# Forget gates of a two-layer attention trunk: which operand stands still, and which PSUM pool takes the result

## The chip, the core and the metric

One core of a Trainium2 chip runs the whole kernel. The metric is the device time of one execution in microseconds (us), of which the median of three runs is given. Engine names are those of the profile: PE is TensorE's matmul, PEld its weight load, DVE is VectorE, ACT ScalarE, POOL GpSimd, SP SyncE, which issues the DMAs.

## What is computed

A trunk of two layers over 2048 tokens with 1024 features. Layer 0 normalises each token, projects it, and runs two groups of attention heads on the result: A (differential attention, four heads) and B (forgetting attention, eight heads). Layer 1 does the same with two other kinds of heads. This case is about the forget gates of B: eight numbers for each token, the last eight columns of layer 0's input projection.

```python
def forgetting_attention(q, k, v, log_f):
    cum = jnp.transpose(jnp.cumsum(log_f, axis=1), (0, 2, 1))
    ...
        s = jnp.einsum("bqhd,bkhd->bhqk", qb, k).astype(jnp.float32) * scale
        s = s + cq[..., :, None] - cum[:, :, None, :]
...
def even_layer(x, ln_g, w_in, w_out, ...):
    z = rms_norm(x, ln_g) @ w_in
    aq, ak, av, ag, bq, bk, bv, bg, bf = split_cols(z, EVEN_SPLITS)   # bf: 8 columns
    ...
    log_f = jax.nn.log_sigmoid(bf.astype(f32) + b_f_bias.astype(f32))
```

## The kernel before, in words

The tokens are cut into 16 blocks of 128 (NT). A block's normalised features are split into a high and a low fp16 half and transposed by DMA, so that `st["x"]` is a tile of 128 features x 16 slices x 128 tokens: slices 0 to 7 (KB is 8) are the high halves, 8 to 15 the low ones. Eight blocks (0, 1, 2, 4, 6, 8, 10, 12; the set RES) stay in SBUF under the name `xr`; the others go to DRAM as `xs` and are loaded back as `x` into two buffers, on SP's queue.

The program is a list of steps, one for each unit (a group of heads) and block. A step has pieces: `p` projects a block (`proj`, L235: 24 matmuls of 512 columns, lines 242 to 244, into the pool `pz`) and ends with `post` (evacuation, norm of q and k, split), `q` multiplies queries and keys (`qk_row`, L322; L339) and `v` multiplies weights and values. `drive` (L842) emits the pieces of neighbouring steps interleaved: `merge` (L47) sorts them by a time that it works out from the cost that each piece carries as a number. From what is emitted, the tile framework's scheduler then makes the order of each engine.

Unit A of head 0 runs first, over the stretch up to about 250 us, while the blocks are still being normalised (`norm_x`, L207), and it alone carries the gates. After the 24 matmuls of a block's projection, `forget` (L736) multiplies the gate weights `wf` (128 features x 8 slices x 16 columns: the high and the low half of eight heads) with the block: for each of the eight slices `wf` is loaded as the 16 stationary columns, and both halves of the block, 256 columns, move. The result, 16 x 256, stands in a tile `psf` of the PSUM pool `pT`. In `post`, `forget_gate` (L745) adds the two halves on DVE (L748, into `fg`, 16 x 128), PE transposes `fg` back into the same PSUM tile (L749), DVE adds the two halves of the weights (L751, into `ff`, 128 x 8), and L752 applies scale and bias. The sixteen results feed `log_gates` (L754) and `cumulate` (L764) some steps later.

Two PSUM pools matter. `pT` has one buffer. It also holds `ptq`, the transposes of q and k that follow in `post` (L277 and L281) and that ACT copies out as `kT` and `qT` (L283 and L286); a tile of this pool can be written only when the one before it has been read. `pS` has two buffers of 1024 columns for the scores `pss` (L339), which DVE adds a bias to and reduces to a minimum (L351, result `mx`). The queue of x is shared with the loads `wrn` of raw weights (L953), whose single buffer ACT must have squared (L176) before the next load starts.

Of the kernel before, what the change touches and what calls it, by code (L numbers as in the profile page):

```python
# [9 lines left out]
F32 = mybir.dt.float32  # L10
# [5 lines left out]
ALU = mybir.AluOpType  # L16
AX = mybir.AxisListType

P = 128
# [3 lines left out]
KB = DM // P  # L23
# [36 lines left out]
class Trunk:  # L60
# [365 lines left out]
    def unit_A(self, h, W, wsc, X):  # L426
        nc, ap = self.nc, self.ap
        ks, vs = [], []

        def mk(tb):  # L430
            st = {}
            m = tb + 1

            def p():
                def z():
                    if "z" not in st:
                        st["z"] = self.pz.tile([P, 512], F32, tag="z", name="z")
                    return st["z"][:]
                pieces = self.proj(st, z, W, 512)
                if h == 0:  # L440
                    pieces.append((KB * 0.107, lambda: self.forget(st)))

                def post():
                    z = self.evac(st["z"], 512, wsc())
                    kd = self.ktile(ks, tb)
                    g = self.qk_prep(st, z, 2, 2, self.gA[h], kd)
                    if h == 0:
                        self.forget_gate(st, tb)
                    next(g)
                    vs.append(self.v_split(z[:, 256:384], wsc(), 1))  # L450
                    st["gate"] = self.silu2(z[:, 384:512], self.subg[:])
                    next(g)
                    st["fin"] = g
                return pieces + [(0.34, post)]
# [35 lines left out]
            def v():  # L490
# [20 lines left out]
                pieces.append((0.0, end))  # L511
                return pieces
            return Step(st, lambda: X(st, tb), p, q, v)
        return [mk(tb) for tb in range(NT)]

# [220 lines left out]
    def forget(self, st):  # L736

        nc = self.nc
        ps = st["f"] = self.pT.tile([P, 512], F32, tag="t", name="psf")
        for kb in range(KB):  # L740
            x = st["x"][:, kb::KB]
            nc.tensor.matmul(ps[0:16, 0:256].rearrange("p (a t) -> p a t", a=2), self.wf[:, kb].rearrange("p a h -> p (a h)"), x,
                             start=(kb == 0), stop=(kb == KB - 1))

    def forget_gate(self, st, tb):  # L745
        nc, ps = self.nc, st["f"]
        g = self.sm.tile([16, P], F32, tag="fg", name="fg", bufs=1)
        nc.vector.tensor_reduce(out=g[:], in_=ps[0:16, 0:256].rearrange("p (a t) -> p t a", a=2), axis=AX.X, op=ALU.add)  # L748
        nc.tensor.transpose(ps[:, 256:272], g[:], self.idf[0:16, 0:16])  # L749
        f = self.sm.tile([P, 8], F32, tag="ff", name="ff", bufs=2)  # L750
        nc.vector.tensor_reduce(out=f[:], in_=ps[:, 256:272].rearrange("p (a h) -> p h a", a=2), axis=AX.X, op=ALU.add)  # L751
        nc.vector.scalar_tensor_tensor(out=self.fy[:, tb], in0=f[:], scalar=self.wfsc[:, 0:1], in1=self.bf[:], op0=ALU.mult, op1=ALU.add)  # L752

    def log_gates(self):  # L754
# [391 lines left out]
```

## Time and profile before

| | us |
|---|---|
| median of 3 runs | 2675.35 (2674.71 to 2675.85) |
| profiled execution | 2674.25 |
| its span in the trace | 2672.5 |
| PE busy | 2357.1 (88%) |
| ACT busy | 1861.9 (70%) |
| DVE busy | 1854.3 (69%) |

The busy shares are averages over the whole program. A view by stretches shows where an engine is full and where it stands idle, and the waits of one stretch say for what. The profiled execution took 1.1 us less than the median; 1.75 us of it lie outside its span.

### The profile page before, as it was taken

How to read it: one execution, taken by the hardware profiler on the slowest of the kernel's cores; microseconds unless marked ns; L12 is line 12 of the kernel's file. 1: busy time of each engine (PE TensorE's matmuls, PEld its weight loads, DVE VectorE, ACT ScalarE, POOL GpSimd, SP SyncE). 2: the span in 40 equal slices, each digit the busy share in tenths (PEclk: the TensorE clock that was granted, in tenths of full speed). 3: DMA queues.
4: the chain of work that ended last, by engine and by line, in shares of the span. 5: the costliest groups of instructions: out<-in, count | busy, mean ns of one | idle time of the engine just before them, and what ended most of it. 6: DMA issues, size and time to landing. Idle time of an engine off the chain costs nothing. (4 is left out here: it accounts for less than half of the span.)

```text
span 2672.5 us, 53354 instructions
## 1 busy us (share of the span) xinstructions
PE 2357.1 (88%) x18448; PEld 1300.2 (49%) x18448; DVE 1854.3 (69%) x5228; ACT 1861.9 (70%) x4289; POOL 1463.9 (55%) x2311
## 2 busy tenths in 40 slices
PE   6778888988889989888995898899999999999799
PEld 2344544545455555445553433565555554555344
DVE  6677888888897867857767544566877676767431
ACT  6676777777777877868777444777987777777420
POOL 4555867777786555645554100656575767576300
PEclk9798999999999999999997999999999999999899
DMA  7756555445356997978879999444666776666983
GB/s 213 185 152 137 123 129 132 96 103 125 93 127 133 186 198 147 210 152 165 169 152 193 268 273 245 144 95 118 146 171 138 174 143 163 142 128 141 247 226 103
DMA packets 888208, 426.67 MB, mean 160 GB/s; under 512 B 785377, under 2 KB 816097, under 8 KB 887937
## 3 DMA queue, kind: packets, MB, share of 16 engines
q1 hardware_dynamic: 887936, 423.27, 69.2%
q8 instruction: 144, 2.36, 0.4%
q14 instruction: 128, 1.04, 0.1%
HBM read 187.68 MB, written 42.01 MB: 86 GB/s over the span
## 5 line engine op out<-in xcount | busy, mean ns | idle before, releaser
L374 ACT ACTIVATE row<-row,mx 128x1024 f32<-128x1024 f32 (+7 forms) x512 | 438.2, 857 | 113.2 <-DVE mx L351 111.1
L339 PE MATMUL pss<-kT,qT 128*128 128x512 f16 (+3 forms) x1728 | 398.1, 347 | 56.3 <-DVE mx L351 49.7
L303 DVE SCALAR_TENSOR_TENSOR ph<-row,ph 128x1024 f16<-128x1024 f32 (+6 forms) x320 | 285.6, 902 | 109.3 <-ACT ph L302 107.3
L242 PE MATMUL z<-w,xr 128*128 128x512 f16 x896 | 346.2, 388 | 16.2 <-DMA xr<-xhl 9.0
L242 PE MATMUL z<-w,x 128*128 128x512 f16 x896 | 342.9, 383 | 11.6 <-DMA x<-xs 10.5
L243 PE MATMUL z<-w,xr 128*128 128x512 f16 x896 | 347.2, 388 | 3.4 <-POOL w L113 1.9
L244 PE MATMUL z<-w,xr 128*128 128x512 f16 x896 | 346.4, 387 | 0.0
L243 PE MATMUL z<-w,x 128*128 128x512 f16 x896 | 342.4, 382 | 0.0
L244 PE MATMUL z<-w,x 128*128 128x512 f16 x896 | 342.2, 382 | 0.0
L121 POOL TENSOR_TENSOR y<-v,mhalf 128x4 f32<-128x4 f32 (+2 forms) x329 | 308.4, 938 | 9.1
L407 PE MATMUL OT<-V,pT 128*128 128x64 f16 x5688 | 237.0, 196 | 79.5 <-DMA pT<-ph 77.4
L407 PEld LDWEIGHTS <-pT 128*128 128x128 f16 x5688 | 215.7, 100 | 147.5 <-DMA pT<-ph 96.9
L302 ACT ACTIVATE ph<-row 128x1024 f16<-128x1024 f32 (+6 forms) x320 | 234.4, 744 | 64.0 <-DMA pT<-ph 59.0
L339 PEld LDWEIGHTS <-qT 128*128 128x128 f16 x1728 | 153.1, 101 | 185.9 <-issue 75.7
L273 POOL TENSOR_TENSOR hl<-zs,hl 128x256 f16<-128x256 f32 (+1 forms) x240 | 177.6, 740 | 101.1 <-ACT hl L272 99.2
L123 DVE TENSOR_TENSOR q<-y 128x4 f32<-128x4 f32 (+2 forms) x329 | 90.6, 276 | 204.3 <-POOL y L121 202.4
L272 ACT ACTIVATE hl<-zs 128x512 f16<-128x512 f32 (+1 forms) x240 | 145.8, 608 | 58.9 <-POOL zs L269 52.9
L250 ACT ACTIVATE zs<-z,sc 128x512 f32<-128x512 f32 (+1 forms) x240 | 158.2, 661 | 25.3 <-PE z L244 25.0
L242 PE MATMUL zo<-w,xm 128*128 128x512 f16 x352 | 137.9, 392 | 31.7 <-DVE res L727 14.0
L176 ACT ACTIVATE wrn<-wrn,lng 128x512 f32<-128x512 f32 (+1 forms) x112 | 78.6, 702 | 108.4 <-DMA wrn<-in_wd_dram 43.3
L497 PE MATMUL OA<-V,pT 128*128 128x128 f16 x1632 | 117.4, 230 | 40.6 <-DMA pT<-ph 34.7
L113 POOL TENSOR_TENSOR w<-wraw,w 128x512 f16<-128x512 f32 x118 | 145.6, 1237 | 11.3 <-ACT w L109 10.6
(225 smaller groups left out, 5562.7 us busy)
## 6 DMA issues: line engine op xcount, KB each, us to landing
x<-xs SPq DMA_DIRECT2D x112, 512.0 KB, 3.8
wraw<-in_w_dram SPq DMA_DIRECT2D x64, 256.0 KB, 3.0
wrn<-in_w_dram SPq DMA_DIRECT2D x56, 256.0 KB, 2.9
x<-in_x_dram SPq DMA_DIRECT2D x16, 512.0 KB, 5.1
xs<-xt SPq DMA_DIRECT2D x16, 512.0 KB, 3.3
mixa<-out SPq DMA_DIRECT2D x128, 64.0 KB, 2.1
biasB<-cumd SPq DMA_DIRECT2D x32, 256.0 KB, 5.1
wrn<-in_wo_dram SPq DMA_DIRECT2D x32, 256.0 KB, 3.3
```

The lines of the kernel that those rows point to most:

```text
L121: nc.gpsimd.tensor_tensor(out=y[:], in0=v[:], in1=self.mhalf[:, :n], op=ALU.pow)
L242: nc.tensor.matmul(ps(), xh, wh, start=(kb == 0), stop=False)
L243: nc.tensor.matmul(ps(), xh, wl, start=False, stop=False)
L244: nc.tensor.matmul(ps(), xl, wh, start=False, stop=(kb == KB - 1))
L250: self.nc.scalar.activation(zs[:, :n], z[:, :n], AF.Copy, scale=sc[:, 0:1])
L272: nc.scalar.activation(hl[:, :, 0::2], zn[:, :, None, :].broadcast_to([P, n, 2, 64]), AF.Copy)
L273: nc.gpsimd.tensor_tensor(out=hl[:, :, 1], in0=zn, in1=hl[:, :, 0], op=ALU.subtract)
L302: nc.scalar.activation(hl[:, :n], w, AF.Copy, scale=scale)
L303: nc.vector.scalar_tensor_tensor(out=hl[:, n:2 * n], in0=w, scalar=scale, in1=hl[:, :n], op0=ALU.mult, op1=ALU.subtract)
L339: nc.tensor.matmul(ps, q()[:, j, :], k[:, slot, (b % 4) * P:(b % 4 + n) * P], start=(j == 0), stop=(j == 1 and not (end and diag)), skip_g ...
L374: nc.scalar.activation(row[:, :hm * P], row[:, :hm * P], AF.Exp, scale=-1.0, bias=nmax, accum_out=s[:, i:i + 1])
L407: nc.tensor.matmul(O[:, head], w()[:, a], V()[:, b], start=first and a + b == 0, stop=last and a == 1, skip_group_check=True)
```

## The change

Stationary and moving operand change places. For each of the 16 slices of a block, the slice itself is loaded as 128 stationary columns (tokens), and the 16 columns of the gate weights move. The result comes out with tokens as rows, 128 x 16, with the sum over both halves of the block made in PSUM. So the first sum on DVE (L748) and the transpose on PE (L749) are gone. The tile `psf` comes from the score pool `pS` in place of `pT`, and the cost with which `merge` places the piece falls from 8 x 0.107 to 8 x 0.056.

```diff
-                    pieces.append((KB * 0.107, lambda: self.forget(st)))
+                    pieces.append((KB * 0.056, lambda: self.forget(st)))
...
     def forget(self, st):
         nc = self.nc
-        ps = st["f"] = self.pT.tile([P, 512], F32, tag="t", name="psf")
-        for kb in range(KB):
-            x = st["x"][:, kb::KB]
-            nc.tensor.matmul(ps[0:16, 0:256].rearrange("p (a t) -> p a t", a=2), self.wf[:, kb].rearrange("p a h -> p (a h)"), x,
-                             start=(kb == 0), stop=(kb == KB - 1))
+        ps = st["f"] = self.pS.tile([P, 16], F32, tag="s", name="psf")
+        for k in range(2 * KB):
+            nc.tensor.matmul(ps[:], st["x"][:, k], self.wf[:, k % KB].rearrange("p a h -> p (a h)"), start=(k == 0), stop=(k == 2 * KB - 1))

     def forget_gate(self, st, tb):
         nc, ps = self.nc, st["f"]
-        g = self.sm.tile([16, P], F32, tag="fg", name="fg", bufs=1)
-        nc.vector.tensor_reduce(out=g[:], in_=ps[0:16, 0:256].rearrange("p (a t) -> p t a", a=2), axis=AX.X, op=ALU.add)
-        nc.tensor.transpose(ps[:, 256:272], g[:], self.idf[0:16, 0:16])
         f = self.sm.tile([P, 8], F32, tag="ff", name="ff", bufs=2)
-        nc.vector.tensor_reduce(out=f[:], in_=ps[:, 256:272].rearrange("p (a h) -> p h a", a=2), axis=AX.X, op=ALU.add)
+        nc.vector.tensor_reduce(out=f[:], in_=ps[:].rearrange("p (a h) -> p h a", a=2), axis=AX.X, op=ALU.add)
         nc.vector.scalar_tensor_tensor(out=self.fy[:, tb], in0=f[:], scalar=self.wfsc[:, 0:1], in1=self.bf[:], op0=ALU.mult, op1=ALU.add)
```

The scheduler makes another order from this, on all engines, over the whole of layer 0; the order of layer 1 stays as it was but for some rows. Lines after the edit stand five lower in the changed file (L742 became L741, L751 became L746, L953 L948, L980 L975).

First place, PE, around the scores of block 2 in unit A (`pss`, 128 x 384, lines 339). Before; what is left out are further matmuls of the same kind:

```order
L742 LDWEIGHTS wf [waits PE_49]
L742 MATMUL psf<-x,wf 16x256 [waits Activation_49]
...
L339 LDWEIGHTS qT
L339 MATMUL pss<-kT,qT 128x384
...
L749 MATMUL psf<-idf,fg 128x16 [waits DVE_49]
L277 LDWEIGHTS hl [waits Pool_49]
L277 MATMUL ptq<-idh,hl 128x128 [waits DVE_49]
```

PE waited at the gate product for ACT (the copy `qT`, which frees `pT`), then ran the scores, then waited for DVE twice, once before each kind of transpose.

The same place in the changed program:

```order
L339 LDWEIGHTS qT [waits Activation_49]
L339 MATMUL pss<-kT,qT 128x384 [waits DVE_49]
...
L277 LDWEIGHTS hl [waits Pool_49]
L277 MATMUL ptq<-idh,hl 128x128 [waits PE_49]
...
L339 MATMUL pss<-kT,qT 128x384 [waits DVE_49]
...
L741 LDWEIGHTS xr
L741 MATMUL psf<-wf,xr 128x16 [waits DVE_49]
...
L497 LDWEIGHTS pT [waits DMAHW3_49]
```

The wait for ACT now stands at the scores, the transposes of the next block stand between the two score products and wait for DVE no more, and the gate product comes behind the scores and waits for DVE, which must have read the score tile whose buffer it takes.

Second place, SP, the loads of two blocks (`x`) in the first third of that unit. Before:

```order
L305 DMA_TRANSPOSE pT<-ph 128x2x128
L953 DMA wrn<-in_w_dram 128x512 x3
L980 DMA x_885<-in_x_dram 128x1024
L980 DMA x_887<-in_x_dram 128x1024
L953 DMA wrn<-in_w_dram 128x512
```

In the changed program:

```order
L305 DMA_TRANSPOSE pT<-ph 128x2x128
L948 DMA wrn<-in_w_dram 128x512
L975 DMA x_905<-in_x_dram 128x1024
L975 DMA x_907<-in_x_dram 128x1024
L948 DMA wrn<-in_w_dram 128x512
```

Two of the three weight loads ahead of the loads of these blocks have moved behind them.

## Rows read from the trace of the kernel before

**Rows 1.** The profile's page: busy time, share of the span and instructions of three engines.

```profile
PE 2357.1 (88%) x18448; PEld 1300.2 (49%) x18448; DVE 1854.3 (69%) x5228; ACT 1861.9 (70%) x4289; POOL 1463.9 (55%) x2311
```

**Rows 2.** The view by stretches: length, then busy time and instructions of PE, PEld, DVE, ACT and POOL, the granted TensorE clock as a share of full speed, DMA share, GB/s.

```profile
20.00:97.00 77.00, 59.71 (x288) 27.65 (x286) 47.36 (x206) 48.73 (x116) 31.74 (x53) 0.84 0.70 192
97.00:250.00 153.00, 117.87 (x764) 62.62 (x765) 112.51 (x316) 102.50 (x231) 90.25 (x135) 0.90 0.66 161
250.00:500.00 250.00, 214.85 (x1477) 120.98 (x1476) 215.14 (x602) 184.26 (x436) 182.36 (x274) 0.95 0.52 121
500.00:1000.00 500.00, 444.14 (x3626) 252.27 (x3625) 412.71 (x1115) 381.45 (x888) 344.86 (x527) 0.98 0.61 134
1000.00:1550.00 550.00, 472.82 (x4468) 263.69 (x4465) 385.68 (x937) 401.47 (x827) 261.99 (x401) 0.95 0.86 183
```

**Rows 3.** The waits of PE from 0 to 270 us: what waited, for whom, total us, times, longest.

```profile
PE psf L742 <- ACT qT L286: 15.1, 9, 4.5
...
PE z L242 <- DMA x<-xs: 10.5, 4, 5.3
PE z L242 <- DMA xr<-xhl: 9.0, 4, 3.9
PE pss L339 <- DVE mx L351: 8.3, 8, 2.1
PE psf L749 <- DVE fg L748: 4.9, 1, 4.9
PE ptq L277 <- DVE ff L751: 3.6, 3, 2.4
...
PE psf L749 <- DVE gt L140: 0.5, 1, 0.5
```

**Rows 4.** Groups by line from 0 to 270 us: line, engine, operation, tiles, shapes, count, then busy us, mean ns of one, and the idle time before them with its releasers.

```profile
L742 PEld LDWEIGHTS <-wf 128*16 128x16 f16 x128 | 11.6, 95 | 23.1 <-issue 18.9 <-PE ptq L281 0.7 <-DVE w L168 0.4
...
L742 PE MATMUL psf<-xr,wf 128*16 128x256 f16 x64 | 9.9, 307 | 8.2 <-ACT qT L286 8.2
...
L742 PE MATMUL psf<-x,wf 128*16 128x256 f16 x64 | 9.1, 290 | 6.9 <-ACT qT L286 6.9
...
L748 DVE TENSOR_REDUCE fg<-psf 16x128 f32<-16x256 f32 x16 | 6.5, 407 | 16.2 <-PE psf L742 16.2
...
L749 PE MATMUL psf<-idf,fg 16*128 16x16 f32 x16 | 3.8, 235 | 5.6 <-DVE fg L748 4.9 <-DVE gt L140 0.5
```

**Rows 5.** The timeline of PE: start, duration, what, and the idle time before it with its releaser. Six gate products lie before 97 us.

```profile
23.79 1.04 PE L742 MATMUL psf<-xr,wf 128*16 128x256 f16 x8
...
50.95 1.04 PE L742 MATMUL psf<-xr,wf 128*16 128x256 f16 x8
...
64.11 1.03 PE L742 MATMUL psf<-xr,wf 128*16 128x256 f16 x8 [0.45 <-ACT qT L286]
...
71.52 1.87 PE L742 MATMUL psf<-x,wf 128*16 128x256 f16 x8 [4.48 <-ACT qT L286]
73.32 1.46 PE L339 MATMUL pss<-kT,qT 128*128 128x384 f16 x4
74.71 0.28 PE L749 MATMUL psf<-idf,fg 16*128 16x16 f32 x1
75.58 0.37 PE L277 MATMUL ptq<-idh,hl 128*128 128x128 f16 x2 [0.59 <-DVE ff L751]
...
77.48 1.86 PE L742 MATMUL psf<-xr,wf 128*16 128x256 f16 x8 [0.46 <-ACT qT L286]
...
85.13 0.61 PE L242 MATMUL z<-w,xr 128*128 128x512 f16 x1 [0.94 <-DMA xr<-xhl]
...
92.44 1.04 PE L742 MATMUL psf<-x,wf 128*16 128x256 f16 x8
...
97.08 0.39 PE L242 MATMUL z<-w,x 128*128 128x512 f16 x1 [1.09 <-DMA x<-xs]
...
201.56 0.28 PE L749 MATMUL psf<-idf,fg 16*128 16x16 f32 x1 [4.91 <-DVE fg L748]
```

**Rows 6.** The timeline of PE at two trains of small matmuls, each with its own load of 128 stationary columns: 24 that move 128 columns, in unit A, and 24 that move 64, in layer 1.

```profile
160.54 1.51 PE L497 MATMUL OA<-V,pT 128*128 128x128 f16 x24 [1.62 <-ACT row L374]
...
1854.90 0.87 PE L407 MATMUL OT<-V,pT 128*128 128x64 f16 x24
```

**Rows 7.** Groups by line, shapes apart, whole span: the means of one such matmul and of one load of 128 columns.

```profile
L407 PE MATMUL OT<-V,pT 128*128 128x64 f16 x5688 | 237.0, 196 | 79.5 <-DMA pT<-ph 77.4 <-DVE out L411 1.4 <-DVE stC L673 0.2
...
L497 PE MATMUL OA<-V,pT 128*128 128x128 f16 x1632 | 117.4, 230 | 40.6 <-DMA pT<-ph 34.7 <-ACT sq L258 4.1 <-ACT row L374 1.6
...
L407 PEld LDWEIGHTS <-pT 128*128 128x128 f16 x5688 | 215.7, 100 | 147.5 <-DMA pT<-ph 96.9 <-issue 6.3
```

**Rows 8.** The timeline of SP's queue: issue, how long until the last of the group was issued, what.

```profile
59.99 7.26 SPq L953 DMA_DIRECT2D wrn<-in_w_dram  x3
67.30 0.90 SPq L980 DMA_DIRECT2D x<-in_x_dram  x2
```

**Rows 9.** The timeline of DVE while PE waited at its longest for the first sum.

```profile
199.33 1.22 DVE L125 SCALAR_TENSOR_TENSOR y<-q,y 128x1 f32<-128x1 f32 x1
200.47 0.15 DVE L474 RECIPROCAL cf<-cf 128x1 f32<-128x1 f32 x1
200.54 0.63 DVE L475 SCALAR_TENSOR_TENSOR cf<-cf,sc,rs 128x1 f32<-128x1 f32 x1
201.10 0.41 DVE L748 TENSOR_REDUCE fg<-psf 16x128 f32<-16x256 f32 x1
```

## The prediction

> **What bounds the kernel now.** I read the page first: PE is busy for 2357.1 of 2672.5 us and no other engine passes 70% [rows 1]. That is an average; the change touches one unit, so the view by stretches comes next [rows 2]. From 20 to 250 us, where all sixteen gate products lie, PE is busy for 59.7 + 117.9 = 178 of 230 us; DVE (160) and ACT (151) are no fuller. No engine is the limit there: the blocks pass through PE, ACT, POOL, DVE and DMA one after another, and PE stands idle for 52 us. After 250 us PE is idle for 14, 11 and 14% of the three stretches, and its own order sets the pace. What comes earlier at 250 us should therefore come earlier at the end.
>
> The waits of PE say what the 52 us are [rows 3]. Three of them belong to the gates: 15.1 us before the gate product for ACT's copy `qT`, 4.9 + 0.5 us before the small transpose, and 3.6 us before the transposes of q and k, which need the buffer that `ff` reads. The rest is mainly DMA (10.5 + 9.0 us for the blocks of x) and 8.3 us in eight waits for DVE to read a score tile. The timeline shows the ring that one `pT` buffer makes [rows 5]: at 71.52 the gate product starts after 4.48 us of waiting, the scores run, the small transpose follows at 74.71, then PE waits again for `ff`, the transposes start at 75.58, and after their copies the next gate product starts at 77.48.
>
> **The change, part by part** (against the profiled 2674.25 us).
>
> (a) The gate products. Before: 9.9 + 9.1 = 19.0 us of PE [rows 4], 1.04 us a block at full clock and 1.87 where PE had just waited [rows 5]. After: 16 pairs of a 128-column load and a matmul with 16 moving columns. The trace has no such pair. The nearest is the train that moves 64 columns with a 128-column load: 24 in 0.87 us, one of them 0.196 [rows 6, 7], so a spacing of (0.87 - 0.196) / 23 = 0.029 us and 15 x 0.029 + 0.196 = 0.64 us a block, 10.2 in all. Gain: 8.8 us. With the 128-column train, (1.51 - 0.230) / 23 = 0.056 us, the block takes 1.06, all blocks 17.0, and the gain is 2.0. With no spacing at all, 16 x 0.196 = 3.1, the gain would be 15.9. At one load's own duration, 0.100 us [rows 7], a block would take 1.70, all of them 27.2: a loss of 8.2. I take the 64-column row, nearest in shape.
>
> (a') Does the load of 128 columns bind? The trace gives the load of `wf`, 16 columns, 95 ns, and a load of 128 columns 100 [rows 4, 7]; and 24 loads of 128 pass in 0.87 us [rows 6], so they overlap each other's recorded time. The Trainium skill (TensorE: Matmul & The Clock Gate, section on LDWEIGHTS) says that a load takes its number of columns divided by 1.2, in ns: some 107 for 128 columns against 13 for 16. That speaks against this change, which loads eight times the columns twice as often; by it the block would take 16 x 0.107 = 1.7 us, an estimate from that page, and (a) would be a loss. The train in the trace speaks against it.
>
> (b) The small transposes: sixteen for 3.8 us [rows 4], and the 5.4 us waited before them. The long one, 4.91 us, was DVE being busy with its queue before it came to `fg` [rows 5, 9]. Gain: 9.2; at the low end, if that queue is met elsewhere, 3.8.
>
> (c) The transposes of q and k no longer wait for `ff`: 3.6 us [rows 3]; low end 0.
>
> (d) The 15.1 us before the gate product: I count 0. The scores that stood right behind need the same copy `qT`, and in the new order the wait stands at them. The far end is the whole 15.1.
>
> (e) New waits. `psf` takes one of two score buffers, so PE waits for DVE's read of the score tile before last, and a later score product waits for `ff`. Where score products wait today, one wait is 8.3 / 8 = 1.04 us [rows 3]. Fourteen blocks have score tiles ahead of them. I take half a wait each, 7 us; ends: 0, and two waits a block, 29. What is queued behind such a wait on PE is the weighted sum of values and the next projection, and ACT and SP wait for those.
>
> (f) Cover. Up to 97 us PE runs into the blocks' DMA [rows 5], so what is saved before that may be waited out at the DMA. Saved there: six gate products, 7.9 - 6 x 0.64 = 4.1; six small transposes, 1.4, with 0.5 of waiting; and 3.6 of (c): 9.6 us. The chain of norms on ACT and DVE also waits for PE's scores, so I give back half, 5 us; ends 0 and 9.6.
>
> (g) Moved loads. Three loads of `wrn` took 7.26 us of SP's queue ahead of two blocks of x [rows 8]; two of them now come later, so the blocks can start up to 4.8 us earlier just where PE waits for them. I take 2 us of gain; ends 0 and 4.8. The two weight loads moved behind are for a later unit and not waited for here.
>
> (h) DVE loses the sixteen sums `fg`, 6.5 us [rows 4]: counted at nothing, since DVE is 70% busy there and PE's waits on it are already in (b), (c) and (e). If DVE were the limit there, it would be worth those 6.5.
>
> (i) The order of units A to B after 250 us is another one, by some rows here and there. PE's idle time from 250 to 1550 us is 35.2 + 55.9 + 77.2 = 168 us [rows 2]. I count 0; that such a shuffle shifts it by 5%, 8 us either way, is an assumption.
>
> Sum: -8.8 - 9.2 - 3.6 + 0 + 7 + 5 - 2 = -11.6 us, so 2662.6 against the profiled time, 2663.8 against the median (1.1 higher). I say 2664.
>
> **The rivals.**
>
> No change. The unit is paced by the blocks' arrival and by `qT`, and only PE work after 97 us counts: the gate products there, 11.1 - 6.4 = 4.8, and ten transposes, 2.4, are eaten by the 7 us of (e). Time: 2675. For it: the largest wait (d) does not vanish, and DMA waits are the next largest. Against: PE is idle only 35 us from 97 to 250, and half of that are waits that the old ring made.
>
> Slower, by the score buffers. If each of the fourteen blocks pays two waits, for its own slot and for the next score tile, (e) is 29 us: -21.6 + 29 + 5 - 2 = +10.4, so 2686. It decides where the waits of a block pass (21.6 - 3) / 14 = 1.3 us. For it: DVE's queue can be 4.9 us behind [rows 5]. Against: today only eight score products wait at all, so the two buffers have slack.
>
> Slower, by the weight loads: pairs spaced by 0.100 us make (a) +8.2 in place of -8.8 and the sum +5.4, so 2681. The train of 24 loads in 0.87 us [rows 6] speaks against it. It is what the section on LDWEIGHTS named above would give.
>
> That the change does not do what it says is excluded by the new order: 256 small pairs, no small transpose, no `fg`.
>
> **How the numbers follow.** A difference under 0.2%, some 5.4 us, cannot be told from none. The forecast has 0.58. No change has 0.22, since (d) and (f) can take everything. The score buffers have 0.12, the weight loads 0.04, and 0.04 goes to an order after 250 us that loses far more than (i). So faster 0.58, same 0.22, slower 0.20. The low end, 2647, is the sum with (e) and (f) at 0 and (g) at 4.8, -26.4, and a little of (i). The high end, 2682, is (a) at 2.0 and (b) at 3.8 with (e) at one wait a block, 14.6: -2.0 - 3.8 - 3.6 + 14.6 + 5 - 2 = +8.2, rounded down to leave the score-buffer case outside.
>
> **What would show it.** Right: sixteen gate blocks of some 0.64 us at full clock; no wait of the transposes on `ff`; waits of the scores on `qT` of 10 us or more in place of the gate product's; waits of `psf` and `pss` on DVE up by some 7 us; the first projection of unit A's second head some 10 us earlier, and the end of layer 0 with it. Wrong: a gate block over 1 us, waits on DVE up by more than 18 us, or a lead at 250 us that is gone by 1550 us.

## The result, and the profile after

The changed kernel takes 2641.5 us (median of four runs; 2635.4 to 2645.9) against 2675.6 for the kernel before beside it, a ratio of 0.9871 (95% interval 0.9849 to 0.9893): 34 us faster. Beside the kernel before on another chip it came out at 0.9877 (0.986 to 0.9895). The forecast was 2664, its low end 2647. The direction was right; the gain was three times the forecast and lay outside the range.

First, where the lead stands. I use two marks on DVE: the first output of unit A's second head (the 17th L508), which closes the unit that carries the gates, and the last output of layer 0's heads (the 64th L411). The first mark, before, in the timeline of DVE (start, duration, what):

```profile
322.92 0.33 DVE L508 SCALAR_TENSOR_TENSOR out<-out,y,gate 128x128 f32<-128x128 f32 x1
```

and in the changed kernel:

```profile
297.03 0.41 DVE L508 SCALAR_TENSOR_TENSOR out<-out,y,gate 128x128 f32<-128x128 f32 x1
```

The lead is 25.9 us there, 21.3 when unit A's last output is made (830.6 and 809.3), 38.5 at the end of layer 0's heads (1498.1 and 1459.6), and 35.3 at the end of the spans (2672.5 and 2637.2). So most of it is made in the first unit, and a second piece late in layer 0, where no instruction was changed.

The gate rows after, groups by line from 0 to 270 us, as in [rows 4]:

```profile
L741 PE MATMUL psf<-wf,xr 128*128 128x16 f16 x128 | 4.9, 171 | 1.3 <-DVE mx L351 1.3
L741 PEld LDWEIGHTS <-xr 128*128 128x128 f16 x128 | 4.7, 98 | 3.3 <-issue 2.1
...
L741 PE MATMUL psf<-wf,x 128*128 128x16 f16 x128 | 4.5, 171 | 1.7 <-DVE mx L351 1.5
...
L746 DVE TENSOR_REDUCE ff<-psf 128x8 f32<-128x16 f32 x16 | 2.7, 167 | 7.9 <-PE psf L741 7.8
```

256 small products take 4.9 + 4.5 = 9.4 us, where 128 took 19.0. The waits of PE from 20 us to the mark at 297 us, which answer to [rows 3] (what waited, for whom, total us, times, longest):

```profile
PE z L242 <- DMA xr<-xhl: 12.1, 5, 6.0
PE OA L497 <- DMA pT<-ph: 9.2, 7, 2.0
PE pss L339 <- DVE mx L351: 8.8, 6, 3.7
PE z L242 <- DMA x<-xs: 6.7, 4, 2.6
PE psn L184 <- ACT qT L286: 5.1, 2, 2.7
PE psf L741 <- DVE mx L351: 2.8, 2, 1.5
PE pss L339 <- ACT qT L286: 2.8, 2, 2.6
PE ptq L277 <- POOL hl L273: 2.6, 1, 2.6
PE z L242 <- ACT w L109: 1.2, 1, 1.2
```

The same view of the kernel before, from 20 us to its mark at 322.9:

```profile
PE psf L742 <- ACT qT L286: 15.1, 9, 4.5
PE z L242 <- DMA x<-xs: 10.5, 4, 5.3
PE OA L497 <- DMA pT<-ph: 9.3, 6, 2.9
PE pss L339 <- DVE mx L351: 8.7, 9, 2.1
PE z L242 <- DMA xr<-xhl: 7.0, 3, 3.9
...
PE ptq L277 <- DVE wt L186: 1.7, 1, 1.7
PE OA L497 <- ACT row L374: 1.6, 1, 1.6
```

The gates' waits are gone, and what stands in their place is smaller: for `qT` 5.1 + 2.8 = 7.9 us in place of 15.1, and 2.8 us of `psf` for a score buffer. The waits for x (17.5 before, 18.8 after), for the score buffers (8.7 and 8.8) and for the transposed weights (9.3 and 9.2) stayed.

The timeline of PE shows how, against [rows 5]:

```profile
54.79 0.55 PE L741 MATMUL psf<-wf,xr 128*128 128x16 f16 x16
...
65.25 0.49 PE L339 MATMUL pss<-kT,qT 128*128 128x384 f16 x2
65.57 0.28 PE L277 MATMUL ptq<-idh,hl 128*128 128x128 f16 x2
65.68 0.39 PE L281 MATMUL ptq<-idh,hl 128*128 128x128 f16 x4
65.91 0.49 PE L339 MATMUL pss<-kT,qT 128*128 128x384 f16 x2
67.67 0.55 PE L741 MATMUL psf<-wf,xr 128*128 128x16 f16 x16 [1.28 <-DVE mx L351]
...
73.36 0.62 PE L741 MATMUL psf<-wf,x 128*128 128x16 f16 x16
...
76.72 0.60 PE L184 MATMUL psn<-wss,onesf 128*128 128x8 f32 x2 [2.74 <-ACT qT L286]
```

Where nothing comes between its pairs, the block of gates takes 0.55 us at a granted clock of 1.00 (54.79) and 0.62 at 0.50 (73.36). At 54.79 it stands between projections and waits for nothing; at 65.57 the transposes of the next block's q and k run between the two score products with no wait for DVE; the one wait for a score buffer in this stretch is 1.28 us. The stretches, as in [rows 2]:

```profile
20.00:97.00 77.00, 58.23 (x365) 28.23 (x364) 54.29 (x233) 55.65 (x132) 42.24 (x68) 0.82 0.75 199
97.00:250.00 153.00, 124.03 (x906) 67.62 (x905) 118.91 (x322) 110.42 (x246) 94.40 (x142) 0.89 0.71 169
250.00:500.00 250.00, 219.38 (x1558) 122.45 (x1555) 216.97 (x626) 184.21 (x452) 187.88 (x288) 0.98 0.53 122
```

DVE, ACT and POOL are busier in each of the first two stretches than before: the work is packed closer.

### The profile page after: what moved, and what is told of

It is laid out like the page before. It is cut to its first block, busy times and chain, and to the rows that moved or that the text cites. A ratio compares the mean times of both kernels' runs of the same rounds, so it can differ in the third digit from the quotient of the medians.

```text
span 2637.2 us, 53573 instructions
## 1 busy us (share of the span) xinstructions
PE 2345.4 (89%) x18560; PEld 1295.5 (49%) x18560; DVE 1851.6 (70%) x5212; ACT 1861.5 (71%) x4289; POOL 1453.8 (55%) x2311
## 3 DMA queue, kind: packets, MB, share of 16 engines
q14 instruction: 127, 1.04, 0.1%
## 4 chain that ended last, share of the span: by engine, by line
PE 23%; DMA 13%; ACT 10%; DVE 9%; POOL 8%; issue 7%; SPq 1%; POOLq 0%; ACTq 0%; DVEq 0%
DMA pT<-ph 6%; PE z L242 3%; PE z L243 3%; PE z L244 3%; PE zo L242 2%; PE OT L407 2%; PE pss L339 2%; PE zo L243 2%; PE zo L244 2%; DVE row L351 2%; ACT ph L302 2%; POOL y L121 2%; DVE ph L303 2%; ACT row L374 2%; DMA wrn<-in_wd_dram 1%
## 5 line engine op out<-in xcount | busy, mean ns | idle before, releaser
L242 PEld LDWEIGHTS <-xr 128*128 128x128 f16 x960 | 95.4, 99 | 117.3 <-DMA xr<-xhl 15.1
L286 ACT ACTIVATE qT<-ptq 128x512 f16<-128x512 f16 (+1 forms) x224 | 144.8, 647 | 8.0 <-PE ptq L281 6.8
```

Of the source, the lines that this page charges most:

```text
L242: nc.tensor.matmul(ps(), xh, wh, start=(kb == 0), stop=False)
```

## The experiments

With the cost number alone changed (0.107 to 0.056) in the kernel before, every row of the order stays as it was on every engine, so that is one program. All other edits of a number gave another order of the whole program, and that became the second question: how much of 34 us is the change, and how much is the order drawn.

### Only the pool

```diff
-        ps = st["f"] = self.pT.tile([P, 512], F32, tag="t", name="psf")
+        ps = st["f"] = self.pS.tile([P, 512], F32, tag="s", name="psf")
```

Expected: 

> The kernel before with one edit: the tile psf comes from the score pool pS; operands, small transpose and both sums stay. The mark is the first output of unit A's second head (DVE L508, the 17th), at 322.9 us before and 297.0 in the changed kernel, a lead of 25.9. Theory 1 (the ring through the one pT buffer cost the first unit its time): the transposes of q and k stop waiting for ff and the gate product stops standing between ACT's copy and the scores, so the mark leads by 12 to 22 us, time 2650 to 2665. Theory 2 (PE's own work, product and transpose, is what was saved): that work is all still there, so the lead is under 5 us, time 2670 to 2680. Theory 3 (the scheduler's new order of later units, by chance): the lead at the mark tells nothing of the total, which can lie 20 us either side of 2675.

Measured: 2654.8 us, ratio 0.9893 (0.9877 to 0.991); mark at 304.5, a lead of 18.4 us. The waits of PE from 20 us to the mark:

```profile
PE pss L339 <- DVE mx L351: 13.7, 7, 4.1
...
PE psn L184 <- ACT qT L286: 3.6, 1, 3.6
PE psf L742 <- DVE mx L351: 3.4, 5, 1.4
PE pss L339 <- DVE ff L751: 3.4, 3, 2.0
...
PE pss L339 <- ACT qT L286: 1.6, 1, 1.6
...
PE psf L749 <- DVE fg L748: 0.7, 2, 0.5
```

No gate work was taken away, and the lead is within what the ring theory said. The waits for `qT` fell from 15.1 to 3.6 + 1.6 = 5.2 us. The price is there too: the buffer is held through the sum, the transpose and the second sum, and `psf` waits 3.4 us for a score buffer, the scores 3.4 us for `ff`. Whether the rise of the scores' waits for DVE's `mx`, from 8.7 to 13.7 us, belongs to it is not shown: in the next run, where `psf` takes no score buffer, they are 14.1.

### Only the operands

The changed kernel with `self.pT.tile([P, 16], F32, tag="t", name="psf")` and the cost at `KB * 0.107`.

Expected: 

> The changed kernel with psf back in pT and the piece's cost back at 0.107: only the operands are swapped, and the small transpose and first sum are gone. Theory 1 (ring): the product is still tied to ACT's copy and the transposes of q and k to ff, so only the shorter block and the missing transpose count, a lead of 8 to 14 us at the mark, time 2660 to 2668. Theory 2 (work): 10 us of product, 3.8 of transposes and the 5.4 us waited before them make most of the lead, 18 to 26 us, time 2645 to 2655. Theory 3 (order by chance): no relation between mark and total.

Measured: 2655.0 us, ratio 0.989 (0.9876 to 0.9905); mark at 305.0, a lead of 17.9 us, between the two theories' figures. Four outputs ahead of the mark and four behind it, it leads by 9.4 and 9.8 us, and over the outputs 33 to 64 by 15 to 23. The waits from 20 us to the mark:

```profile
PE pss L339 <- DVE mx L351: 14.1, 8, 3.4
PE psf L741 <- ACT qT L286: 13.0, 4, 4.5
...
PE pss L339 <- ACT qT L286: 3.0, 1, 3.0
```

With the old pool the wait for `qT` stays: 13.0 + 3.0 us. So it is the pool, not the shorter product, that took this wait away. The two halves do not add up (18.4 + 17.9 is more than 25.9); each is one order, and the next runs show how far an order alone moves the mark, so the two leads do not size the halves.

### The same work in other orders

Six kernels change a number that places pieces and nothing else: the gate piece's cost in the changed kernel back at 0.107, that cost at 0.16 in the kernel before, and the evacuation piece of unit A at 0.30 and 0.45 in each.

```diff
-                return pieces + [(0.34, post)]
+                return pieces + [(0.30, post)]
```

Cost back at 0.107, expected: 

> The changed kernel with the piece's cost back at 0.107: the same instructions, another order from the scheduler, in layer 1 too. Theories 1 and 2: the mark leads by 20 to 31 us as in the changed kernel, and the total lies within 10 us of 2641. Theory 3 (order by chance): the total differs from 2641 by 10 us or more, in whatever units the order differs.

Cost 0.16 in the kernel before, expected: 

> The kernel before with the piece's cost at 0.16 in place of 0.107: the same instructions as before, another order from the scheduler, in layer 1 too. Theories 1 and 2: mark within 5 us of 322.9, time within 8 us of 2675. Theory 3 (order by chance): the total moves by 10 us or more either way though no work has changed.

0.30 in the kernel before, expected: 

> The kernel before with the number that places the evacuation piece of unit A at 0.30 in place of 0.34: the same instructions, a third order of the scheduler for the work before. Theory 3 with what the cost of 0.16 gave (9 to 22 us less with no work changed): the order before was a poor draw, and this one too comes out 5 to 25 us under the kernel before. Theories 1 and 2 alone: within 8 us of it.

0.30 in the changed kernel, expected: 

> The changed kernel with the same number at 0.30: a third order for the changed work. If the change is worth some 10 us over draws of the order, the three draws of the changed work (the changed kernel, cost 0.107, this) lie 5 to 15 us under the three of the work before on average, and overlap. If it is worth 25 us (theories 1 and 2 alone), all three lie 20 us or more under the kernel before and none overlaps with a draw of the work before.

0.45 in the kernel before, expected: 

> The kernel before with the number of unit A's evacuation piece at 0.45: a fourth order for the work before. If the change itself is worth 22 us at the mark over draws of the order, the mark lies within 12 us of 322.9, as in the other three (322.9, 311.1, 325.0). The stretch from the mark to the end of layer 0 lies between 1150 and 1176 us, as in the draws so far, with no relation to the kind of gates.

0.45 in the changed kernel, expected: 

> The changed kernel with the same number at 0.45: a fourth order for the changed work. If the change is worth 22 us at the mark, it lies within 5 us of 297.7, as in the other three (297.0, 298.5, 297.5). From the mark to the end of layer 0: 1150 to 1176 us.

The changed kernel again, expected: 

> The changed kernel once more, beside the kernel before on this chip. If a session's chip moves both alike, the ratio comes out at 0.985 to 0.989 again, and the mark within 2 us of 297.0.

Measured (the rest is the profiled span less the mark; ratios are to the kernel before on the same chip, whose median was 2675.6 to 2684.2 us in the four sessions, so totals compare by their ratios):

| work | order | mark | rest | median | ratio (95%) |
|---|---|---|---|---|---|
| before | as it was | 322.9 | 2349.6 | 2675.6 | 1 |
| before | gate cost 0.16 | 311.1 | 2354.3 | 2662.0 | 0.9919 (0.990 to 0.9939) |
| before | 0.30 | 325.0 | 2343.0 | 2669.9 | 0.9971 (0.9956 to 0.9985) |
| before | 0.45 | 312.5 | 2351.1 | 2665.5 | 0.9940 (0.9924 to 0.9956) |
| changed | as it is | 297.0 | 2340.2 | 2641.5 | 0.9871 (0.9849 to 0.9893) |
| changed | the same again | 295.7 | 2352.0 | 2648.1 | 0.9877 (0.986 to 0.9895) |
| changed | gate cost 0.107 | 298.5 | 2351.2 | 2654.0 | 0.9890 (0.9873 to 0.9906) |
| changed | 0.30 | 297.5 | 2340.8 | 2642.7 | 0.9871 (0.9847 to 0.9896) |
| changed | 0.45 | 301.5 | 2361.7 | 2664.4 | 0.9939 (0.9922 to 0.9955) |

Three things follow. The first unit separates the two kinds of work: the marks lie at 311 to 325 us in four orders of the old gates (mean 317.9) and at 297 to 301.5 in four of the new (mean 298.6; the second run of the changed kernel has 295.7), with no overlap, 19 us apart. The mark is a favourable place: the first projection of unit A's second head, a sign that the prediction named, starts at 233.3 and 218.4 us in the mean, 15 us apart and again without overlap, and over the outputs 33 to 64 the means lie 15 to 19 us apart. The rest of the program does not separate them: 2343.0 to 2354.3 against 2340.2 to 2361.7, with equal means (2349.5, and 2350.0 with the two runs of one program averaged). And the order before was the slowest of four that compute the same: other numbers alone gave it 0.3 to 0.8%.

So the change is worth some 15 to 19 us; the mean ratios, 0.9958 and 0.9894, differ by 0.64%, 17 us. An estimate from the scatter of the four orders gives these differences a standard error of 4 us at the mark and 6 us in all. The other half of the 34 us is a poor order before and a good one after: 6.6 us of the lead at the mark (25.9 less 19.3) and 9.4 us behind it. The granted clock does not sort the rests: 0.965 stands beside 2340.8 (changed, 0.30) and 0.956 beside 2343.0 (before, 0.30). At 0.45 the two kinds take the same time in all, though their marks are 11 us apart.

Against the expectations: that the old work would keep its mark within 5 us and its time within 8 at cost 0.16 did not hold: the mark came 11.8 us earlier and the time was 0.8% less. The lead at cost 0.107, 24.4 us, and the marks at 0.45 and of the second run came out as expected. After three orders of each kind no ratio of one overlapped with one of the other, as the larger worth would have it; the fourth pair, at 0.45, brought them together.

### The same order, without the scheduler

Both kernels with `schedule_with_timeline_sim=False`: the program's own order. On PE it is one and the same from some 550 us on; over the second head too it still differs, where the expectation says that only the first unit differs.

The kernel before, expected: 

> The kernel before without the framework's scheduler: every engine runs its instructions in the order in which the program emits them. No theory says what this costs in all; it is the other half of the pair with n2. Its own first unit ends somewhere near 320 us (first output of unit A's second head).

The changed kernel, expected: 

> The changed kernel without the scheduler. Against n1 only the rows of the first unit differ; from row 4602 of PE's 36486 others on, the two stand in one order, so chance has no hand in it after the first unit. Theory 1 with 2 (the change itself saves time in the first unit): a lead over n1 of 8 to 20 us at the first output of the second head, kept to the end, so 8 to 20 us less in all. Theory 3 (what the changed kernel gained came from the scheduler's order): a lead under 5 us, and a total within 6 us of n1.

Measured: 3232.6 us (3216.2 to 3239.6) and 3212.0 (3205.9 to 3225.1); marks at 314.7 and 305.6, a lead of 9.1 us, 9.0 at unit A's last output (8.7 to 13.7 at each output between), 13.7 at the end of the spans (3237.0 and 3223.3) and 20 between the medians, which scatter by as much. The waits of PE from 20 us to the mark, in the kernel before:

```profile
PE z L242 <- DMA xr<-xhl: 21.4, 4, 11.8
PE ptq L277 <- POOL hl L273: 17.3, 8, 5.6
...
PE psf L742 <- ACT qT L286: 8.4, 5, 5.9
PE psf L749 <- DVE fg L748: 6.0, 4, 2.5
```

and in the changed one:

```profile
PE ptq L277 <- POOL hl L273: 28.3, 12, 4.8
PE psf L741 <- DVE mx L351: 20.2, 7, 6.5
PE z L242 <- DMA xr<-xhl: 13.5, 3, 11.3
```

Here the score buffers do cost: `psf` waits 20.2 us for DVE, where the scheduled orders of the changed work have 2.4 to 5.5. The lead is half as large as over those orders; since the transposes wait 11 us more for POOL as well, how much of that the buffers account for is not shown. The rival with the score buffers is real in this order.

### No gates at all

The changed kernel without the calls of `forget` and `forget_gate`, and the following line, so that the gates' logits are a constant:

```diff
+        nc.vector.memset(self.fy[:], 3.0)
```

Expected: 

> The changed kernel without gate products: their sixteen blocks on PE and the sums on DVE are left out, and the tile that should take the gates' logits holds a constant. On PE the rows of later units of layer 0 stand in the changed kernel's order. It says what the gates still cost after the change. If their cost is PE's work alone, the mark (first output of unit A's second head, 297.0 in the changed kernel) leads by 9 us more, the sixteen blocks of 0.55 us. If score buffers still cost (the waits of psf on DVE, 2.8 us, and of score products held up behind), 12 to 18 us more. If the blocks' DMA waits take it back, under 5 us more. From the mark to the end of layer 0, as in the changed kernel, within 5 us of its 1162.6 us.

Measured: 2661.1 us, 0.9933 (0.9916 to 0.995), which is 13 us more than the changed kernel on the same chip. Its mark lies at 299.0, 2 to 3 us behind the changed kernel's. The waits of PE from 20 us to the mark:

```profile
PE OA L493 <- DMA pT<-ph: 20.4, 9, 4.6
PE pss L339 <- DVE mx L351: 11.0, 6, 4.8
PE z L242 <- DMA xr<-xhl: 11.0, 4, 4.9
```

With the gates gone, PE waits 20.4 us for the transposed weights in place of 9.2. So in this order taking the gates away gave the first unit no further lead: the 9 us of PE's work that were left out came back as waits. It is one order, another than the changed kernel's up to some 285 us, and 2 to 3 us are what orders alone do to the mark (297.0 to 301.5), so a gain of some us in other orders is not excluded. Of the three cases expected the third comes nearest, but the wait that grew is that for the transposed weights, not that for the blocks of x. The end of layer 0's heads lies at 1464.1 against 1465.1 for the changed kernel in the same session; the orders on PE are one from 285 to 1400 us. The 13 us are lost behind that, where the order is another one: the next output lies at 1694.6 against 1686.4, and from it to the end the span has 963.9 against 961.3 us.

## Why the prediction was wrong, point by point

(a) The products: forecast 8.8 us less; 19.0 to 9.4, 9.6 less. The row it was taken from was the right one: (0.55 - 0.171) / 15 = 0.025 us a pair, against 0.029 for 64 columns. Part of the gain is that the new block hardly feels the clock: three of the old ones ran at a granted clock of 0.50, the lower of the two levels (1.2 GHz), and took 1.87 us in place of 1.04, where a new one at 0.50 took 0.62 in place of 0.55.

(a') The rival with the weight loads is refuted: sixteen loads of 128 columns and their products pass in 0.55 us. The section on LDWEIGHTS of the page TensorE: Matmul & The Clock Gate in the Trainium skill would have a load of 128 columns take some 107 ns. The recorded load, 98 ns, is near that, but the trace does not agree that such a load spaces the pairs, at 25 ns each.

(b), (c) 9.2 and 3.6 us: the small transposes, the waits before them and the waits for `ff` are all gone, as forecast. (What the transposes of q and k wait for in their place stands under (f), (g).)

(d) is the step that failed. I counted nothing for the 15.1 us before the gate product, since "the scores that stood right behind need the same copy `qT`". That did not hold: the scores wait 2.8 us for `qT`. Once the product does not need the `pT` buffer, PE has other work to run while ACT copies, and the waits for `qT` fell to 7.9 us: 7.2 less. The other 5.1 us of them stand before `psn` (L184, the norms of weights), which takes the `pT` buffer itself. The two halves of the change show the cause: 5.2 us with only the pool changed, 16.0 with only the operands. The orders bear it out: the old gates wait 13.3 to 16.1 us at the product, and the programs with the new ones 5.2 to 7.9 us for `qT` in all. The far end of 15.1 stood in the text but was not carried into the range.

(e) was mis-sized: 7 us forecast, 2.9 measured (2.8 of `psf`, 0.1 more of `pss`). How much it costs depends on the order: `psf` waits 20.2 us in the program's own.

(f), (g) Forecast as 3 us lost in all. From the waits of both kernels up to the mark: x costs 1.3 us more; new waits for POOL, ACT and DVE 2.6 + 1.2 + 0.6 + 0.2 (2.8 of them before the transposes of q and k); 3.3 us of old waits for `wt` and `row` are gone, and 0.1 of those for the transposed weights: 2.5 us lost. The loads of two blocks of x did move, from 67.30 [rows 8] to 61.53 us in the timeline of SP's queue, and the projection of the first of them, the seventh block, from 85.13 [rows 5] to 80.84:

```profile
61.53 1.06 SPq L975 DMA_DIRECT2D x<-in_x_dram  x2
...
80.84 0.61 PE L242 MATMUL z<-w,xr 128*128 128x512 f16 x1 [1.38 <-DMA xr<-xhl]
```

Together, -9.6 - 9.2 - 3.6 - 7.2 + 2.9 + 2.5 = -24.2 us, against a lead of 25.9 at the mark; the 1.7 us between are busy time of PE's other matmuls. This adds up PE's time, busy and waiting, in one pair of orders: it says where the time went, not what each term would be worth alone. Without the gates, 9 us less of PE's work gave no lead, in the one order that was run.

(i) failed too, by its size. The order behind 250 us was counted at nothing, with 8 us either way. Behind the mark the orders spread over 2340 to 2362 us, and this pair drew 9.4 us in its favour (2349.6 and 2340.2). The text did not reckon that the order before could itself be a poor draw, already in the first unit: its mark is 5 us later than the mean of four. The same changed program in another session had 2352.0 for its rest, so part of the 9.4 may not be the order at all. With the 7.2 us of (d) in it, the forecast would have been some 2657, still inside the range; the draw of the orders, half of the 34 us, is what carried the time below 2647.

The rivals: "no change" is refuted by the marks; the score buffers and the weight loads as above. The forecast of the change itself, 11.6 us, compares with 15 to 19 over orders and 9 in the program's own, so the direction was no luck; half of the 34 us is the luck of the two orders. What stays open is which rows of the order make the rest longer or shorter; no run took these apart.

## What to carry to other kernels

A wait before an instruction that holds a single buffer is not certain to move to the next instruction that needs the same data: look whether the engine gains other work to run meanwhile when the buffer is no longer asked for, and carry both ends into the range. Where a scheduler redraws the whole order on every edit, measure a change as several orders of each version, with a number that moves pieces and no work; here that spread was 0.8%, more than the 0.64% that the change is worth. A mark right behind the changed stage tells the change from the draw, and several marks are better than one: here they gave 15 to 19 us.

## What the runs showed of the hardware

At a granted clock of 1.00, a matmul that moves 16 columns with its own load of 128 stationary ones follows the one before it after 25 ns, where one that moves 64 took 29 [rows 6]: a quarter of the columns saved 4 ns. At a granted clock of 0.50, a block of 16 such pairs took 0.62 us (73.36) in place of 0.55, while 8 matmuls that move 256 columns took 1.87 in place of 1.04 [rows 5]. And the recorded load takes 98 ns for 128 columns and 95 for 16 [rows 4].

How far one program's times spread differs from session to session: 2674.7 to 2676.1 for the kernel before beside 2635.4 to 2645.9 for the changed kernel, and 2672.6 to 2686.3 for the kernel before in the next session.
